# Moving matmul operands to 512-byte boundaries, joining a tile's scans, and spacing the convolution

## The chip, the cores and the metric

One core of a Trainium2 chip runs the whole program. The metric is the device time of one execution in microseconds, the median of three runs. Five engines work side by side: TensorE (PE; its weight loads are listed apart as PEld), VectorE (DVE), ScalarE (ACT), GpSimd (POOL) and SyncE (SP), which only issues DMAs here. A matmul has a stationary operand, which a weight load brings into the array, and a moving operand, which streams past it; both are read from SBUF. An address in SBUF is a byte offset inside each of the 128 partitions.

## The reference, cut to what matters

The layer is two SwiGLU feed-forward blocks around a mixer, on 256 tokens of 2048 channels, all in float32:

```python
x = x + 0.5 * swiglu(rms_norm(x, g1), w1, w3, w2)      # w1, w3: 2048x5632, w2: 5632x2048
h = rms_norm(x, gm);  p = h @ w_in                     # q|k, v, o, gates, u
qk = silu(causal_depthwise_conv(qk, conv_w, conv_b))   # 4 taps, 1024 channels
hm = mlstm_chunkwise(q, k, v, i, f);  hm = rms_norm(hm) * sigmoid(o)
bu = einsum('bsgh,gph->bsgp', u, b_bar)                # 64 groups of 16 channels, 64 states each
states = associative_scan(combine, (lam_bar, bu))      # s[t] = lam_bar * s[t-1] + bu[t]
y = gelu(real(einsum(states, c)) + d * u);  hs = y * sigmoid(y @ w_glu + b_glu)
x = x + concat(hm, hs) @ w_out
x = x + 0.5 * swiglu(rms_norm(x, g2), v1, v3, v2)
out = rms_norm(x, gf)
```

## The kernel before

Every large product is done in three matmuls on pairs of float32r numbers. A weight tile arrives as float32 in `wraw`; ACT rounds it to `whi` (line 154), DVE forms the rest `wlo = wraw - whi` (line 156), and activations are split the same way into `xh`/`xl`, `gh`/`gl`, `hmh`/`hml`, `yh`/`yl` and `hsh`/`hsl`. The product is then hi·hi + hi·lo + lo·hi.

The work is cut into weight steps. One step is 512 KB of weights (two blocks of 128 rows by 512 columns) and one call of `step_tok` or a quarter to an eighth of `gemm_ch`. In `step_tok` (line 174) the activation is stationary and the weight is moving: 12 matmuls of 512 columns. In `gemm_ch` (lines 224 to 226) the weight is stationary and the activation moves, 256 columns at a time: 24 matmuls. Three steps are prepared ahead (`AHEAD`), through four `wraw`, three `whi` and three `wlo` buffers.

The stages in order: feed-forward 1 (`w1`, `w3` from `xh`/`xl`, then `w2` from `gh`/`gl`, in two halves of 6 and 5 chunks), the mixer, feed-forward 2 in the same form. The last column block of the last `w2` is done by `tail`, with 256-column matmuls on lines 474 to 476. The mixer's products are, in order: `u` (two chunks, `gemm_ch`), `o` and the gates (three chunks of 344 columns), `q|k` (two chunks, `gemm_ch`), `v` (two chunks), the first half of `w_out` from `hmh`/`hml`, `w_glu` from `yh`/`yl` (`gemm_ch`), and the second half of `w_out` from `hsh`/`hsl`.

Beside the products of the mixer runs the S5 branch, in eight tiles of four scan rows. Each tile is six tasks: load (DMAs of its tables on SP's queue), drive (16 small matmuls, then four DVE products by the rotation table and two POOL sums), scan (line 860), unrotate (six POOL operations, lines 868 to 873), emit (matmuls and one DVE operation), act (ACT and DVE). The tasks wait in the list `self.bg`; after each weight step `tick` runs 0.62 of one on average (`S5_RATE`). The convolution and other short pieces are put in by `self.after(n, fn)`: `fn` is recorded after the n-th weight step from then. SP's order is the recorded one; the order on the other engines is made by a scheduler from the recorded program.

The tiles lie one after another in SBUF, in the order in which the pools are opened, so each tile's address follows from the sizes of those before it. As the two programs are built, the starts of TensorE's operands, modulo 512 bytes, are:

| operand | where it is used | before | changed |
|---|---|---|---|
| `xh`, `xl` | stationary in `w1`, `w3`, `o`, `v`; moving in `u`, `q\|k` | 256 | 0 |
| `whi`, `wlo` | moving in `step_tok` and `tail`, stationary in `gemm_ch` | 256 | 0 |
| `gh`, `gl` | stationary in `w2` and `tail` | 320 | 0 |
| `hsh`, `hsl` | stationary in the second half of `w_out` | 352 | 0 |
| `hmh`; `hml` | stationary in the first half of `w_out` | 32; 96 and 0 | 0 |
| `yh`, `yl` | moving in `w_glu` | 352 | 0 |

Within a tile the slices step by 512 or 1024 bytes in the stationary operand and by 1024 or 2048 in the moving one (1376 in the 344-column chunks, whose second block so starts at 96 before). `xh` and `whi` lie below byte 96,000 of a partition; all the other operands of the table lie above 114,000, before and after.

Of the kernel before, what the change touches and what calls it, by code (L numbers as in the profile page):

```python
# [8 lines left out]
F32 = mybir.dt.float32  # L9
# [28 lines left out]
AHEAD = 2  # L38
WARM = 7
# [20 lines left out]
class _Layer:  # L60
# [172 lines left out]
    def setup(self):  # L233
# [16 lines left out]
        vec0 = self.junkp.tile([KD, P], F32, name="vec0")  # L250
# [3 lines left out]
        idle = self.junkp.tile([P, NC], F32, name="junk")  # L254
# [8 lines left out]
        self.mhalf = c.tile([P, 8], F32, name="mhalf")  # L263
# [6 lines left out]
        vecs = self.junkp.tile([rows, P], F32, name="vecs")  # L270
# [500 lines left out]
    def mixer(self, chunk_done):  # L771
# [4 lines left out]
        with ExitStack() as ctx:  # L776
            mp = self.pool("mix", ctx=ctx)
# [7 lines left out]
            def make_rB():  # L785
                b = self.bank()
                for t in range(TT):
                    dg = tp2.tile([P, P], F32, name="dg")
                    V.tensor_scalar(dg, self.ident, rstd(t), None, op0=ALU.mult)
                    nc.tensor.matmul(b[:, t * P:(t + 1) * P], lhsT=self.ones, rhs=dg, start=True, stop=True)  # L790
# [5 lines left out]
            uT = [mp.tile([P, 4, 2, HC], F32, name=f"uT{i}", tag=f"uT{i}") for i in range(2)]  # L796
            u4 = [mp.tile([P, 8, HC], F32, name=f"u4{i}", tag=f"u4{i}") for i in range(2)]
# [14 lines left out]
            yT = mp.tile([P, NJ, S], F32, name="yT")  # L812
            yh = mp.tile([P, NJ, S], F32R, name="yh")
            yl = mp.tile([P, NJ, S], F32R, name="yl")
# [7 lines left out]
            def s5(j):  # L822
# [3 lines left out]
                def load():  # L826
# [9 lines left out]
                    Bt = [mp.tile([P, 4, HC], F32, name=f"B{i}") for i in range(2)]  # L836
                    env["t"] = rv, w1, w2, k0, At, Bt

                def drive():
                    rv, w1, w2, k0, At, Bt = env["t"]  # L840
# [15 lines left out]
                def scan():  # L856
                    rv, w1, w2, k0, At, Bt = env["t"]
                    for a in (0, 2):
                        for q in range(4):
                            V.tensor_tensor_scan(At[a + 1][:, q, :],  # L860
                                                 self.R[:, 4 * j + q:4 * j + q + 1].broadcast_to([P, HC]),
                                                 At[a][:, q, :], 0.0, op0=ALU.mult, op1=ALU.add)

                def unrotate():
                    rv, w1, w2, k0, At, Bt = env["t"]
                    cs, sn = rv[:, 0], rv[:, 1]
                    zr, zi = At[1], At[3]
# [7 lines left out]
                def emit():  # L875
                    rv, w1, w2, k0, At, Bt = env["t"]
# [51 lines left out]
            for i, part in enumerate(self.gates(mp, gt, Dm, em)):  # L928
# [24 lines left out]
            for hf in range(2):  # L953
                acc = self.pair()
                self.gemm_ch(acc, self.xs, win, KD, QK0 + hf * NC)
                qkp[hf] = mp.tile([P, 4, S + 3], F32, name=f"qkp{hf}", tag=f"qkp{hf}")
# [4 lines left out]
                for i in range(4):  # L961
                    self.after(1 + i, lambda hf=hf, i=i: conv(hf, i))
# [37 lines left out]
            def heads_T(c):  # L1000
                hmh[c] = mp.tile([P, 4, S], F32R, name=f"hmh{c}", tag=f"qkp{c}")
                hml[c] = mp.tile([P, 4, S], F32R, name=f"hml{c}", tag=f"vx{c}")
# [15 lines left out]
            for c in range(2):  # L1018
                v = mp.tile([P, TT, 2, DV + 1], F32, name=f"vx{c}", tag=f"vx{c}")
# [37 lines left out]
            hsh = [mp.tile([P, 4, S], F32R, name=f"hsh{i}", tag=f"uT{i}") for i in range(2)]  # L1057
            hsl = [mp.tile([P, 4, S], F32R, name=f"hsl{i}", tag=f"u4{i}") for i in range(2)]
# [26 lines left out]
    def gates(self, mp, gt, Dm, em):  # L1085
# [3 lines left out]
        rows = mp.tile([H, 4, S], F32, name="g_rows", tag="vx1")  # L1089
        more = mp.tile([H, 4, S], F32, name="g_more", tag="qkp1")  # L1090
        E = mp.tile([H, NCK, S], F32, name="g_E", tag="vx0")
# [130 lines left out]
```

## Time and profile before

| | |
|---|---|
| median of 3 runs | 1885.29 us (1884.81 to 1885.33) |
| the profiled execution | 1883.44 us, of which the profile's span is 1881.7 us |
| PE busy | 1840.2 us, 9221 matmuls |
| DVE busy | 1082.8 us, 1335 instructions |
| ACT, POOL busy | 811.5 us, 340.3 us |
| clock granted to TensorE | 0.995 of full speed on average |

A matmul's duration in the profile runs to the modelled end of its pipeline, so consecutive matmuls overlap and a busy PE may still be slower than it could be. What a matmul costs in a dense stretch is the time from its start to the next one's start; the timeline gives it.

### The profile page before, as it was taken

The page shows a single profiled execution, that of the slowest core. Times are in us where ns is not written, and L with a number is a line of the kernel's source. Part 1 is how long each engine was busy: PE and PEld are TensorE (multiplying, and loading weights), DVE is VectorE, ACT ScalarE, POOL GpSimd, SP SyncE. Part 2 cuts the span into 40 slices and gives each one's busy share as a digit, 9 for nine tenths or more (in the row PEclk, how much of TensorE's full clock was granted, in tenths as well). Part 3 has the DMA queues.
Part 4 walks back from the last instruction along what each step waited for, and adds up shares of the span by engine and source line. Part 5 has one row for each costly group of instructions (what it writes and reads, how often), then busy time and mean ns, then how long its engine had stood idle before and what let it go on. Part 6 is the DMA issues. An engine that isn't in the chain of part 4 may idle for free.

```text
span 1881.7 us, 24161 instructions
## 1 busy us (share of the span) xinstructions
PE 1840.2 (98%) x9221; PEld 1539.7 (82%) x9221; DVE 1082.8 (58%) x1335; ACT 811.5 (43%) x970; POOL 340.3 (18%) x523
## 2 busy tenths in 40 slices
PE   9999999999999999988889999999999999999998
PEld 7888888888888888987778888888888888888887
DVE  5547865555555455577888765445444444444454
ACT  6444443334444444434544455444443334444343
POOL 3000999700000000166323200000000000000011
PEclk9999999999999999999999999999999999999999
DMA  8666666666666555776766556666665566666554
GB/s 261 190 189 188 200 208 216 236 197 201 189 194 197 186 194 189 206 156 179 158 155 178 168 178 204 190 190 190 190 190 185 187 188 190 190 190 190 190 188 148
DMA packets 191252, 358.27 MB, mean 190 GB/s; under 512 B 12320, under 2 KB 29344, under 8 KB 191008
## 3 DMA queue, kind: packets, MB, share of 16 engines
q1 hardware_dynamic: 186992, 344.58, 62.2%
q0 software_dynamic: 4000, 11.10, 1.8%
q8 instruction: 72, 1.18, 0.3%
q10 hardware_dynamic: 144, 1.05, 0.1%
q14 instruction: 44, 0.36, 0.1%
HBM read 344.62 MB, written 11.01 MB: 189 GB/s over the span
## 4 chain that ended last, share of the span: by engine, by line
PE 48%; DVE 5%; issue 1%; DMA 1%; ACT 1%; POOL 0%; ACTq 0%; POOLq 0%; DVEq 0%
PE accb L174 42%; DVE wlo L156 2%; DVE A L860 1%; PE accb L226 1%; PE accb L224 1%; PE accb L225 1%; DMA wraw<-in_w_in_dram 1%; DVE qkc L942 1%; PE tpb L486 1%; PE accb L474 0%; PE accb L476 0%; PE accb L475 0%; DVE qkc L939 0%; ACT whi L154 0%; PE tpb L845 0%
## 5 line engine op out<-in xcount | busy, mean ns | idle before, releaser
L156 DVE TENSOR_TENSOR wlo<-wraw,whi 128x1024 fp32r<-128x1024 f32 (+1 forms) x630 | 788.6, 1254 | 736.6 <-ACT whi L154 736.0
L154 ACT CAST whi<-wraw 128x1024 fp32r<-128x1024 f32 (+1 forms) x630 | 655.0, 1041 | 950.9 <-PE accb L174 856.9
L174 PE MATMUL accb<-wlo,xh 128*128 128x512 f32 (+1 forms) x1568 | 606.2, 387 | 17.1 <-DVE wlo L156 17.1
L174 PE MATMUL accb<-whi,xh 128*128 128x512 f32 (+1 forms) x1568 | 609.7, 389 | 0.0
L174 PE MATMUL accb<-whi,xl 128*128 128x512 f32 (+1 forms) x1568 | 605.6, 387 | 0.0
L174 PEld LDWEIGHTS accb<-wlo,xh 128*128 128x128 f32 x1568 | 296.0, 189 | 76.4 <-DVE wlo L156 20.1
L174 PEld LDWEIGHTS accb<-whi,xl 128*128 128x128 f32 x1568 | 296.2, 189 | 57.9
L174 PEld LDWEIGHTS accb<-whi,xh 128*128 128x128 f32 x1568 | 295.9, 189 | 58.0 <-ACT whi L154 1.1
L174 PE MATMUL accb<-whi,gh 128*128 128x512 f32 x664 | 263.7, 397 | 0.0
L174 PE MATMUL accb<-whi,gl 128*128 128x512 f32 x664 | 262.4, 395 | 0.0
L174 PE MATMUL accb<-wlo,gh 128*128 128x512 f32 x664 | 262.3, 395 | 0.0
L174 PEld LDWEIGHTS accb<-whi,gl 128*128 128x128 f32 x664 | 124.7, 188 | 30.2
L174 PEld LDWEIGHTS accb<-whi,gh 128*128 128x128 f32 x664 | 124.7, 188 | 29.7
L174 PEld LDWEIGHTS accb<-wlo,gh 128*128 128x128 f32 x664 | 124.7, 188 | 29.6
L1186 POOL TENSOR_TENSOR x<-x,fn 128x512 f32<-128x512 f32 x6 | 8.9, 1500 | 699.6 <-ACT junk L317 699.6
L696 POOL TENSOR_TENSOR tr<-s5rot,sp 128x128 f32<-128x128 f32 (+6 forms) x112 | 62.1, 555 | 151.9 <-DVE sp L636 148.4
L226 PE MATMUL accb<-xh,wlo 128*128 128x256 f32 x256 | 73.6, 288 | 6.6 <-DVE wlo L156 6.6
L224 PE MATMUL accb<-xh,whi 128*128 128x256 f32 x256 | 73.9, 289 | 0.0
L225 PE MATMUL accb<-xl,whi 128*128 128x256 f32 x256 | 73.0, 285 | 0.0
L757 POOL DMA_DIRECT2D spillw<-s5w x16 | 8.6, 541 | 274.6 <-ACT s5w L728 259.7
L697 POOL TENSOR_TENSOR tr<-s5rot,sp 128x128 f32<-128x128 f32 (+6 forms) x112 | 57.8, 517 | 0.0
L226 PEld LDWEIGHTS accb<-xh,wlo 128*128 128x128 f32 x256 | 49.6, 194 | 7.6 <-DVE wlo L156 7.6
(312 smaller groups left out, 1416.3 us busy)
## 6 DMA issues: line engine op xcount, KB each, us to landing
wraw<-in_ffn_w_dram SPq DMA_DIRECT2D x528, 512.0 KB, 3.7
wraw<-in_w_in_dram SPq DMA_DIRECT2D x48, 512.0 KB, 5.3
wraw<-in_w_out_dram SPq DMA_DIRECT2D x32, 512.0 KB, 3.7
wraw<-in_w_in_dram SPq DMA_DIRECT2D x24, 344.0 KB, 5.6
spillrot<-s5rot POOLq DMA_DIRECT2D x8, 512.0 KB, 5.3
spillw<-s5w POOLq DMA_DIRECT2D x16, 256.0 KB, 4.2
s5rot<-spillrot SPq DMA_DIRECT2D x8, 512.0 KB, 7.8
wraw<-in_w_glu_dram SPq DMA_DIRECT2D x8, 512.0 KB, 3.9
```

Source lines behind the costliest of these rows:

```text
L154: nc.scalar.copy(hi, raw)
L156: nc.vector.tensor_sub(lo, raw, hi.bitcast(F32))
L174: nc.tensor.matmul(acc[t][:, :n], lhsT=x, rhs=wt, start=first and t not in seen, stop=last and t not in left)
L224: nc.tensor.matmul(o, lhsT=wh[:, kk, ns], rhs=xh, start=st, stop=False, **kw)
L225: nc.tensor.matmul(o, lhsT=wh[:, kk, ns], rhs=xl, start=False, stop=False, **kw)
L226: nc.tensor.matmul(o, lhsT=wl[:, kk, ns], rhs=xh, start=False, stop=sp, **kw)
L486: nc.tensor.transpose(b[:, o:o + P], s[t][:, kt * P:(kt + 1) * P], self.ident)
L696: G.tensor_tensor(tr[0][:, :, :k], rv[:, 0, :, 0:k], u0, op=ALU.mult)
L697: G.tensor_tensor(tr[1][:, :, :k], rv[:, 1, :, 0:k], u1, op=ALU.mult)
L860: V.tensor_tensor_scan(At[a + 1][:, q, :], self.R[:, 4 * j + q:4 * j + q + 1].broadcast_to([P, HC]), At[a][:, q, :], 0.0, op0=ALU.mult, op ...
L942: V.scalar_tensor_tensor(o, src[:, w:w + S], self.col("conv_w", w * 8 + j), o, op0=ALU.mult, op1=ALU.add)
L1186: nc.gpsimd.tensor_tensor(self.x[c][:, t, :], self.x[c][:, t, :], self.fn[:, c * NC:(c + 1) * NC], op=ALU.mult)
```

## The change

All operands of TensorE in the table above are moved to addresses that are whole multiples of 512. Small paddings (`mhalf`, `junk`) shift the early pools; two early vectors move from the junk pool into S5 buffers; in the mixer a pool `ma` for the operands is opened first, the tiles `qkp` and `vx`, whose buffers later hold `hmh` and `hml`, are padded to 1152 numbers, and the rest goes to `mp`. The S5 tile's scan becomes one instruction over its four rows, in place, with a tile `Rt` as the multiplier that ACT fills in the load task and whose first column in each row is zero, so that a row starts anew. Unrotate takes the two freed tiles as its scratch, and `B0`, `B1` go. The convolution's four tiles of a chunk are recorded after weight steps 1, 3, 5, 7 and not 1, 2, 3, 4.

```diff
+WIDE = 1152
...
-        vec0 = self.junkp.tile([KD, P], F32, name="vec0")
+        vec0 = self.s5p.tile([KD, P], F32, name="vec0", tag="s5k0")
...
-        idle = self.junkp.tile([P, NC], F32, name="junk")
+        idle = self.junkp.tile([P, NC + 112], F32, name="junk")[:, :NC]
...
-        self.mhalf = c.tile([P, 8], F32, name="mhalf")
+        self.mhalf = c.tile([P, 72], F32, name="mhalf")[:, :8]
...
+            ma = self.pool("mixa", ctx=ctx)
             mp = self.pool("mix", ctx=ctx)
...
-            uT = [mp.tile([P, 4, 2, HC], F32, name=f"uT{i}", tag=f"uT{i}") for i in range(2)]
+            uT = [ma.tile([P, 4, 2, HC], F32, name=f"uT{i}", tag=f"uT{i}") for i in range(2)]
...
+            Rt = [mp.tile([P, 4, HC], F32, name=f"Rt{i}") for i in range(2)]
+            for i in range(2):
+                G.memset(Rt[i][:, :, 0:1], 0.0)
...
-                    Bt = [mp.tile([P, 4, HC], F32, name=f"B{i}") for i in range(2)]
-                    env["t"] = rv, w1, w2, k0, At, Bt
+                    A.copy(Rt[j % 2][:, :, 1:],
+                           self.R[:, 4 * j:4 * j + 4].unsqueeze(2).broadcast_to([P, 4, HC - 1]))
+                    env["t"] = rv, w1, w2, k0, At
...
                     for a in (0, 2):
-                        for q in range(4):
-                            V.tensor_tensor_scan(At[a + 1][:, q, :],
-                                                 self.R[:, 4 * j + q:4 * j + q + 1].broadcast_to([P, HC]),
-                                                 At[a][:, q, :], 0.0, op0=ALU.mult, op1=ALU.add)
+                        x = At[a].rearrange("p q c -> p (q c)")
+                        V.tensor_tensor_scan(x, Rt[j % 2].rearrange("p q c -> p (q c)"), x, 0.0,
+                                             op0=ALU.mult, op1=ALU.add)
...
-                    zr, zi = At[1], At[3]
+                    zr, zi, Bt = At[0], At[2], (At[1], At[3])
...
-                qkp[hf] = mp.tile([P, 4, S + 3], F32, name=f"qkp{hf}", tag=f"qkp{hf}")
+                qkp[hf] = ma.tile([P, WIDE], F32, name=f"qkp{hf}", tag=f"qkp{hf}")[:, :4 * (S + 3)].rearrange("p (j s) -> p j s", j=4)
...
-                    self.after(1 + i, lambda hf=hf, i=i: conv(hf, i))
+                    self.after(1 + 2 * i, lambda hf=hf, i=i: conv(hf, i))
```

TensorE's order is that of before. On DVE the first place is the second chunk of `q|k`, where the convolution of the first chunk stands between the `wlo` steps; `qkc` is written by a convolution tile's four operations, and `yT` is S5's emit. Before:

```order
L156 TENSOR_TENSOR wlo_8061<-wraw_8057,whi_8059 128x1024
L939 TENSOR_SCALAR qkc_7626<-qkp0_7972,cols_130 128x256
L888 SCALAR_TENSOR_TENSOR yT_6406<-uT0_6402,cols_130,tpb_8092 128x256
L942 SCALAR_TENSOR_TENSOR qkc_7626<-qkp0_7972,cols_130,qkc_7626 128x256
L156 TENSOR_TENSOR wlo_8115<-wraw_8111,whi_8113 128x1024
L942 SCALAR_TENSOR_TENSOR qkc_7626<-qkp0_7972,cols_130,qkc_7626 128x256
L939 TENSOR_SCALAR qkc_7626<-qkp0_7972,cols_130 128x256
L942 SCALAR_TENSOR_TENSOR qkc_7626<-qkp0_7972,cols_130,qkc_7626 128x256 x2
L156 TENSOR_TENSOR wlo_8150<-wraw_8146,whi_8148 128x1024
```

The same place on DVE in the changed program:

```order
L157 TENSOR_TENSOR wlo_8082<-wraw_8078,whi_8080 128x1024
L945 TENSOR_SCALAR qkc_7605<-qkp0_7950,cols_130 128x256
L157 TENSOR_TENSOR wlo_8117<-wraw_8113,whi_8115 128x1024
L948 SCALAR_TENSOR_TENSOR qkc_7605<-qkp0_7950,cols_130,qkc_7605 128x256
L945 TENSOR_SCALAR qkc_7605<-qkp0_7950,cols_130 128x256
L948 SCALAR_TENSOR_TENSOR qkc_7605<-qkp0_7950,cols_130,qkc_7605 128x256 x3
L157 TENSOR_TENSOR wlo_8153<-wraw_8149,whi_8151 128x1024
```

Between the three `wlo` steps there stood two and four operations of the convolution, and now one and five; the next steps have four, none and two.

On ACT the second place is the end of the second `u` chunk: the casts of that chunk (128x1024) and of the first `o` chunk (128x688). Before:

```order
L340 ACTIVATE xh_6479<-tpb,cols 128x256 x4
L154 CAST whi<-wraw 128x1024 x11
L154 CAST whi<-wraw 128x688 x8
L892 ACT_TABLE_LOAD
L892 ACTIVATE yT<-yT 128x256
```

And in the changed program, where `Rt` is the scan's multiplier:

```order
L341 ACTIVATE xh_6486<-tpb,cols 128x256 x4
L155 CAST whi<-wraw 128x1024 x11
L842 COPY Rt_6416<-R 128x4x127
L155 CAST whi<-wraw 128x688 x7
L842 COPY Rt_6417<-R 128x4x127
L155 CAST whi<-wraw 128x688
L898 ACT_TABLE_LOAD
```

The third of the eight copies into `Rt` stands in front of the casts of the `o` chunk; it writes the buffer that the first tile's scan on DVE reads, and the casts behind it follow in order.

## Rows read from the trace of the kernel before

**Rows 1.** page: span, busy time, clock and GB/s by slices, chain by engine

```profile
span 1881.7 us, 24161 instructions
...
PEclk9999999999999999999999999999999999999999
...
GB/s 261 190 189 188 200 208 216 236 197 201 189 194 197 186 194 189 206 156 179 158 155 178 168 178 204 190 190 190 190 190 185 187 188 190 190 190 190 190 188 148
...
PE 48%; DVE 5%; issue 1%; DMA 1%; ACT 1%; POOL 0%; ACTq 0%; POOLq 0%; DVEq 0%
```

**Rows 2.** groups by shape on PE: line, operands, count; busy us, mean ns; idle

```profile
L174 PE MATMUL accb<-whi,xh 128*128 128x512 f32 x1472 | 577.4, 393 | 0.0
...
L174 PE MATMUL accb<-whi,gh 128*128 128x512 f32 x664 | 263.7, 397 | 0.0
...
L174 PE MATMUL accb<-whi,hsh 128*128 128x512 f32 x64 | 25.6, 400 | 0.0
...
L474 PE MATMUL accb<-whi,gh 128*128 128x256 f32 x48 | 13.3, 276 | 0.0
...
L474 PE MATMUL accb<-xh,gh 128*128 128x256 f32 x32 | 8.8, 276 | 0.0
```

**Rows 3.** timeline of PE (start, us, engine, line), feed-forward 2, w1 and w3

```profile
1169.79 0.39 PE L174 MATMUL accb<-whi,xl 128*128 128x512 f32 x1
...
1171.15 0.39 PE L174 MATMUL accb<-whi,xl 128*128 128x512 f32 x1
```

**Rows 4.** timeline of PE, feed-forward 2, w2

```profile
1499.72 0.40 PE L174 MATMUL accb<-whi,gh 128*128 128x512 f32 x1
...
1501.12 0.40 PE L174 MATMUL accb<-whi,gh 128*128 128x512 f32 x1
```

**Rows 5.** timeline of PE, tail

```profile
1859.81 0.28 PE L475 MATMUL accb<-wlo,gh 128*128 128x256 f32 x1
...
1860.49 0.28 PE L475 MATMUL accb<-xl,gh 128*128 128x256 f32 x1
```

**Rows 6.** timeline of PE, u chunk (gemm_ch)

```profile
774.81 0.28 PE L225 MATMUL accb<-xl,whi 128*128 128x256 f32 x1
...
775.53 0.28 PE L225 MATMUL accb<-xl,whi 128*128 128x256 f32 x1
```

**Rows 7.** timeline of PE after its longest wait in the v chunk

```profile
975.12 0.63 PE L174 MATMUL accb<-whi,xl 128*128 128x512 f32 x1
...
976.82 0.63 PE L174 MATMUL accb<-whi,xh 128*128 128x512 f32 x1
```

**Rows 8.** windows: stretch, us, PE busy (count), granted clock, DMA share, GB/s

```profile
974.50:977.00 2.50, 2.48 (x6) 0.50 0.42 66
```

**Rows 9.** waits of PE in 785 to 985 us: total us, times, longest

```profile
PE accb L174 <- DVE wlo L156: 16.3, 9, 5.1
PE accb L226 <- DVE wlo L156: 6.6, 5, 2.9
```

**Rows 10.** windows: stretch, us, busy of PE, PEld, DVE, ACT, POOL, clock

```profile
920.00:980.00 60.00, 48.32 (x328) 41.93 (x328) 54.41 (x82) 27.89 (x35) 24.65 (x18) 0.94 0.53 137
```

**Rows 11.** groups by shape on DVE, 760 to 1110 us

```profile
L860 DVE TENSOR_TENSOR_SCAN A<-R,A 128x128 f32<-128x128 f32 x64 | 36.7, 636 | 2.6 <-POOL A L853 2.6
...
L1115 DVE TENSOR_TENSOR_SCAN g_rows<-g_more,g_rows 4x256 f32<-4x256 f32 x1 | 0.7, 678 | 0.0
```

**Rows 12.** timeline of POOL: end of the first unrotate

```profile
815.13 1.79 POOL L873 TENSOR_TENSOR S<-B,B 128x512 f32<-128x512 f32 x1
```

**Rows 13.** timeline of DVE: first scans, and the second drive

```profile
802.97 4.79 DVE L860 TENSOR_TENSOR_SCAN A<-R,A 128x128 f32<-128x128 f32 x8
...
818.36 0.68 DVE L849 TENSOR_TENSOR A<-tpb,s5rot 128x512 f32<-128x512 f32 x1
```

**Rows 14.** groups by shape on ACT: a copy of 128x512

```profile
L724 ACT COPY s5w<-tpb 128x512 f32<-128x512 f32 x8 | 4.6, 579 | 0.0
```

**Rows 15.** timeline of ACT: first cast of the o chunk

```profile
805.23 0.77 ACT L154 CAST whi<-wraw 128x688 fp32r<-128x688 f32 x1 [1.83 <-PE accb L225]
```

More of the change, by code (lines that the diff above doesn't have):

```diff
@@ L269, in setup @@
         rows = 16 + 16 + 32 + 8 * 4
-        vecs = self.junkp.tile([rows, P], F32, name="vecs")
+        vecs = self.s5p.tile([rows, P], F32, name="vecs", tag="s5k0")
         r = 0
@@ L793, in mixer @@
             self.after(7, make_rB)
-            uT = [mp.tile([P, 4, 2, HC], F32, name=f"uT{i}", tag=f"uT{i}") for i in range(2)]
-            u4 = [mp.tile([P, 8, HC], F32, name=f"u4{i}", tag=f"u4{i}") for i in range(2)]
+            uT = [ma.tile([P, 4, 2, HC], F32, name=f"uT{i}", tag=f"uT{i}") for i in range(2)]
+            u4 = [ma.tile([P, 8, HC], F32, name=f"u4{i}", tag=f"u4{i}") for i in range(2)]
             def evac_u(hf, acc):
@@ L927, in mixer @@
             em = mp.tile([P, TT, H], F32, name="em")
-            for i, part in enumerate(self.gates(mp, gt, Dm, em)):
+            for i, part in enumerate(self.gates(ma, mp, gt, Dm, em)):
                 self.after(1 + 4 * i, part)
@@ L1000, in heads_T @@
             def heads_T(c):
-                hmh[c] = mp.tile([P, 4, S], F32R, name=f"hmh{c}", tag=f"qkp{c}")
-                hml[c] = mp.tile([P, 4, S], F32R, name=f"hml{c}", tag=f"vx{c}")
+                hmh[c] = ma.tile([P, 4, S], F32R, name=f"hmh{c}", tag=f"qkp{c}")
+                hml[c] = ma.tile([P, 4, S], F32R, name=f"hml{c}", tag=f"vx{c}")
                 for half in range(2):
@@ L1054, in mixer @@
             self.drain_bg()
-            hsh = [mp.tile([P, 4, S], F32R, name=f"hsh{i}", tag=f"uT{i}") for i in range(2)]
-            hsl = [mp.tile([P, 4, S], F32R, name=f"hsl{i}", tag=f"u4{i}") for i in range(2)]
+            hsh = [ma.tile([P, 4, S], F32R, name=f"hsh{i}", tag=f"uT{i}") for i in range(2)]
+            hsl = [ma.tile([P, 4, S], F32R, name=f"hsl{i}", tag=f"u4{i}") for i in range(2)]
             def evac_glu(hf, acc):
@@ L1083, in mixer, with gates @@
                 chunk_done(c)
-    def gates(self, mp, gt, Dm, em):
+    def gates(self, ma, mp, gt, Dm, em):
         nc = self.nc
         V, G, A = nc.vector, nc.gpsimd, nc.scalar
-        rows = mp.tile([H, 4, S], F32, name="g_rows", tag="vx1")
-        more = mp.tile([H, 4, S], F32, name="g_more", tag="qkp1")
-        E = mp.tile([H, NCK, S], F32, name="g_E", tag="vx0")
+        rows = ma.tile([H, 4, S], F32, name="g_rows", tag="vx1")
+        more = ma.tile([H, 4, S], F32, name="g_more", tag="qkp1")
+        E = ma.tile([H, NCK, S], F32, name="g_E", tag="vx0")
         li, f, bc, M = (rows[:, i, :] for i in range(4))
```

18 lines of the change are left out of this document (9 added, 9 removed).

## The prediction

> **What bounds the kernel now.** I read the page first: the chain of waits gives PE 48% of its own and hardly anything to the others, and TensorE's clock is granted in full in all forty slices [rows 1]. So outside the mixer only two things can shorten the program, fewer matmuls or matmuls that follow each other sooner; PE's order and its number of matmuls stay. Then I took the groups of PE by shape, for the counts [rows 2], and the timeline of PE in dense stretches, for the time from one matmul's start to the next one's, which is what a matmul costs there.
>
> At the full clock of 2.4 GHz, 512 columns at one column a cycle would take 213.3 ns and 256 columns 106.7 ns. The timeline shows more, and not the same everywhere. Stationary `xh`/`xl` with moving weights: six matmuls in 1171.15 - 1169.79 = 1.36 us, 226.7 ns each [rows 3]. Stationary `gh`/`gl`: six in 1.40 us, 233.3 ns [rows 4]. The tail, 256 columns on `gh`: six in 0.68 us, 113.3 ns [rows 5]. `gemm_ch`, 256 columns: six in 0.72 us, 120 ns [rows 6]. At the half clock there is no excess: four matmuls in 1.70 us are 425 ns, against 512/1.2 = 426.7 ns [rows 7, 8]. So at the full clock something costs 13.3 or 20 ns a matmul, and it differs with the operands. That is what this change can act on.
>
> Last I read the waits of PE in the mixer: between 785 and 985 us it waits 16.3 + 6.6 us for `wlo` of DVE [rows 9], DVE being busy 54.4 of the 60 us from 920 on while the granted clock falls to 0.94 [rows 10]. There, and only there, what DVE does counts.
>
> **The change part by part.** The sum is made against the profiled 1883.44 us; the median is 1885.29, so 1.85 are added at the end.
>
> *Operands that are in step already.* In `w1`, `w3` and `v` both operands start at 256 modulo 512, in `gemm_ch` of `u` and `q|k` too; afterwards both start at 0. Two readings of the rows are possible. By the first, the excess depends on how the stationary start stands to the moving start: 256 against 256 costs 13.3 ns, `gh` at 320 against weights at 256 costs 20. Then 0 against 0 is 256 against 256, and the 4416 matmuls (3 x 1472 [rows 2]) stay at 226.7. By the second, the excess is paid for operands that do not start on a line of 512, and it goes. Ends: 0 and -13.3 x 4416 = -58.9 us; for `gemm_ch`, 768 matmuls (4 chunks x 8 steps x 24), 0 and -10.2. I take 0 for both. The reason is the tail beside `gemm_ch`: the tail's stationary start, 320, is out of step with the moving 256 and it has the shorter distance, 113.3 against 120, while with 512 columns out of step is the longer. Being off the line is common to all four rows, so it cannot make the difference between them; the pairing can.
>
> *Operands that come into step.* `gh`/`gl`, 3 x 664 = 1992 matmuls of 512 columns [rows 2], go from 320 against 256 to 0 against 0, so by the first reading from 233.3 to 226.7: -6.7 x 1992 = -13.3 us. Ends: 0 (the difference comes from where in SBUF `gh` lies, above byte 114,000, which it keeps) and -20 x 1992 = -39.8 (the second reading). `hsh`/`hsl`, 3 x 64 = 192, and `hmh`/`hml`, also 192 and partly on the line already, have no dense rows of their own; out of step like `gh`, I give them its price, and half of it for `hm`, where one tile starts at 0: -1.3 and -0.6; ends 0 and -20 x 384 = -7.7. The tail, 3 x (48 + 32) = 240 matmuls of 256 columns [rows 2], goes the other way by this reading, from 113.3 to the 120 of the pairs in step: +1.6; other end -1.6. `yh` in `w_glu` (192) and the three chunks of 344 columns, whose second block started at 96, I leave at 0; other end about -7 ns x 192 and, at 13.3 ns, 288 matmuls of the latter: -5.2 together.
>
> *Scans.* Now eight scans a tile, 64 in all with a mean of 636 ns; the first eight stand in one row of 4.79 us [rows 11, 13]. Afterwards two of 512 elements. The only longer scan, 256 elements, took 678 ns [rows 11]; twice that for 512 is 1.36, so two take 2.7 us if nothing else holds them. But a scan of 128 elements should take less than the 256-element one by far more than 636 against 678 shows: part of the mean is waiting inside the instruction, which I expect to remain. Ends per tile: 0 and 4.79 - 2.7 = -2.1 us of DVE, over eight tiles -16.6 of DVE's time. Of that only what lies ahead of a late `wlo` reaches PE, at most the 22.9 us of waits [rows 9] together with the next part. I take 0.
>
> *Copies into `Rt`.* Eight on ACT, each near the 128x512 copy of 579 ns [rows 14]: 4.6 us of an engine that is busy 27.9 of 60 us [rows 10]. But the third stands in front of the casts of the `o` chunk and must wait until the first tile's scans have read the buffer; they ended at 802.97 + 4.79 = 807.76, and the first of these casts started at 805.23 [rows 13, 15]. It would be late by 2.5 us, plus the copy. Queued behind it are `whi`, then `wlo`, then PE, with three steps prepared ahead, each of 12 matmuls of 344 columns here. I take 0 for all; the price without this cover is a rival below. Unrotate's scratch is now `At[1]` and `At[3]`, so the next drive waits for POOL's last read of them: before, POOL ended at 815.13 + 1.79 = 816.92 and the drive's first product started at 818.36 [rows 12, 13], 1.4 us to spare. Cost 0; if the cover goes, what POOL is late by, at most a microsecond or two a tile.
>
> *Convolution.* Four tiles of four operations go to every second step. In the second `q|k` chunk DVE has one, five, four, none and two of them between `wlo` steps where it had two, four, four, one and one: nearly the same clumps. The fourth tile goes where steps are empty, and in the `v` chunk, which holds the longest wait [rows 9], tasks of S5 stand beside it. Ends: +3 (the longer clump) and half of the 22.9 us of waits, -11.5. I take -4, a third of the better end, since one tile in four changes its place by much.
>
> Sum: -13.3 - 1.3 - 0.6 + 1.6 - 4 = -17.6; 1883.4 - 17.6 = 1865.8, and with 1.85 as a median 1867.7. Forecast: 1868 us.
>
> The supply of weights does not stop this: a step of 512 KB in 12 x 213.3 ns = 2.56 us wants 205 GB/s, and the first slice moved 261 [rows 1].
>
> **A rule of the Trainium skill.** The page "TensorE: Matmul & The Clock Gate", section "Back-to-back issue gap", gives N/2.4 + 2.5 ns for a matmul alone at the full clock: 215.8 ns for 512 columns and 109.2 for 256. The trace disagrees, with 226.7 and 233.3, 120 and 113.3 [rows 3 to 6]; if the excess over that rule is what alignment costs, rival A would end near 1785 instead of the time worked out for it below. The page "SBUF — State Buffer", section "Specifications (TRN2)", gives lines of 16 bytes and a penalty for each crossing. All the starts of before are multiples of 16, so by it moving them is worth nothing, which is rival C; the difference of 226.7 and 233.3 between two multiples of 16 speaks against it.
>
> **The rivals.**
> A: the line decides, and on it the whole excess goes. FFN with `xh`, 4224 x 13.3 = 56.3 (4416 less the 192 of `v`); `gh` 39.8; `hs` 3.8; tail 1.6; in the mixer, where PE waits for DVE in part, I count about 8 of the 17 to 20 that the ends above allow; with the convolution 113.5. 1883.4 - 113.5 + 1.85 = 1772. For it: no excess at the half clock, so reading cannot keep up, as it would with split lines. Against it: 256 columns out of step are quicker than in step.
> B: half of the excess goes, one operand's share: (109.5)/2 + 4 = 59, so 1826.
> C: what differs is the place in SBUF, or nothing in the starts; then only the convolution acts: 1885.3 - 4 = 1881, and 1885 if that does nothing either. For it: `xh` lies low and `gh` high.
> S, slower: the copies into `Rt` hold the casts. The third to eighth each wait for the scan of two tiles before, up to 2.5 us, and all take ACT's time: 6 x 2.5 + 8 x 0.58 = 19.6 us. If half of it reaches PE and the starts give nothing, 1885.3 + 9.8 = 1895. It decides as soon as a copy is later than the three prepared steps last, 12 matmuls of 344 columns each; PE's waits for `wlo` show that this lead is often used up already [rows 9].
>
> **How the numbers follow.** Forecast 0.45, A 0.22, B 0.10, C 0.12, S 0.11. The measurement can tell about 0.2% from no change, 3.8 us. Faster: forecast, A, B and a quarter of C, 0.80; same: most of C, 0.09; slower: S, 0.11. The range goes from A's 1772 to C's 1884; left out are S and the far side of A. The forecast's own range is 1860 to 1876, from the ends of the convolution and of `hs`, `hm` and the tail.
>
> **What will show it.** In the timeline of PE: `gh` at 226.7 ns and `xh` still at 226.7 is the forecast; both at about 213 is A, both near 220 B, 233 and 227 C. The tail at 120 or 113 tells whether pairing or being out of step matters at 256 columns. In the mixer: the waits for `wlo` between 785 and 985 us below 20 us, the scan's mean by shape near 2.3 us if the waiting inside it remains and 1.4 if not, and the cast after the third copy no later than before. The forecast is wrong if `xh` changes its distance, and wrong in the other way if `whi` waits for `Rt`.

## The result and the profile after

The changed kernel took 1860.21 us, the median of 4 runs (1858.73 to 1863.14), against 1885.31 for the kernel before on the same chip (4 runs, 1884.81 to 1887.8). The ratio is 0.9868, with a 95% interval of 0.9856 to 0.9880: 1.3% faster, 25.1 us where 17.3 were forecast. The execution that was profiled took 1863.14 us, 20.3 less than that of before.

From the page of the changed kernel, each engine's busy time in us, its share of the span and its instructions:

```profile
PE 1828.1 (98%) x9221; PEld 1540.8 (83%) x9221; DVE 1077.2 (58%) x1287; ACT 814.8 (44%) x977; POOL 347.6 (19%) x525
```

PE has the same 9221 matmuls. Where the time went is read by stages. This table is worked out from the starts in both traces: from a stage's first matmul to the first of the next, in us.

| stage | before | after | difference |
|---|---|---|---|
| feed-forward 1 and 2, `w1`/`w3` (four stretches) | 272.12, 224.79, 266.53, 221.23 | 272.79, 224.77, 266.48, 221.17 | +0.5 |
| `w2` without the tail (four stretches) | 137.52, 117.77, 135.28, 84.88 | 133.85, 114.77, 131.45, 82.49 | -12.9 |
| tail | 27.10 | 28.67 | +1.6 |
| `u` | 51.52 | 50.34 | -1.2 |
| `o` and gates, 344 columns | 68.92 | 69.64 | +0.7 |
| `q\|k` | 67.71 | 61.71 | -6.0 |
| `v` | 65.14 | 63.76 | -1.4 |
| first half of `w_out`; `w_glu`; second half | 54.47; 23.03; 47.58 | 53.56; 23.03; 46.23 | -0.9; 0; -1.4 |

The timeline of PE in the dense stretches of the changed kernel (start and duration in us), in the order `u`, `w1`/`w3`, `w2`, tail:

```profile
774.76 0.28 PE L226 MATMUL accb<-xl,whi 128*128 128x256 f32 x1
...
775.48 0.28 PE L226 MATMUL accb<-xl,whi 128*128 128x256 f32 x1
...
1169.88 0.39 PE L175 MATMUL accb<-whi,xl 128*128 128x512 f32 x1
...
1171.24 0.39 PE L175 MATMUL accb<-whi,xl 128*128 128x512 f32 x1
...
1479.88 0.39 PE L175 MATMUL accb<-whi,gl 128*128 128x512 f32 x1
...
1481.24 0.39 PE L175 MATMUL accb<-whi,gl 128*128 128x512 f32 x1
...
1840.04 0.28 PE L475 MATMUL accb<-xh,gh 128*128 128x256 f32 x1
...
1840.76 0.28 PE L475 MATMUL accb<-xh,gh 128*128 128x256 f32 x1
```

Each pair spans six matmuls. `xh` takes 1.36 us, 226.7 ns each, as before [rows 3]. `gh` takes 1.36 where it took 1.40 [rows 4], so 226.7 and not 233.3. The tail takes 0.72 where it took 0.68 [rows 5], 120 and not 113.3 ns, and `gemm_ch` 0.72 as before [rows 6]. This holds for whole stages and not only for the pairs shown. Worked out from all starts in both traces, without the distances that hold a wait, the means are: `w2` 233.3 before and 226.8 after, `w1`, `w3` and the other products of `xh` 226.9 in both, the tail 113.4 and 120.0.

In the mixer, the waits of PE in 785 to 985 us (us in all, times, the longest):

```profile
PE accb L175 <- DVE wlo L157: 14.6, 12, 3.4
...
PE accb L175 <- ACT whi L155: 1.5, 3, 0.8
PE accb L227 <- DVE wlo L157: 1.4, 4, 0.8
```

Against [rows 9] the waits for `wlo` fell from 22.9 to 16.0 us, 5.2 of it in `gemm_ch` (6.6 to 1.4), and a small wait for `whi` is new. The groups of DVE in 760 to 1110 us hold the scans:

```profile
L867 DVE TENSOR_TENSOR_SCAN A<-Rt,A 128x512 f32<-128x512 f32 x16 | 28.7, 1820 | 2.6 <-POOL A L860 2.6
```

They keep DVE busy for 28.7 us and not 36.7 [rows 11]. The means hide two kinds of scan. The shortest, median and longest in ns, before and after:

```profile
L860 DVE TENSOR_TENSOR_SCAN A<-R,A x64: 391/394/1518, 803.0 to 1039.8; 128x128 f32<-128x128 f32 x64
L867 DVE TENSOR_TENSOR_SCAN A<-Rt,A x16: 1192/2282/2317, 796.6 to 1024.1; 128x512 f32<-128x512 f32 x16
```

Of the 64 scans before, 14 took 1.44 to 1.52 us and nearly all others 0.39 to 0.42. Of the 16 joined ones, 9 took 2.27 to 2.32 and the others 1.19 to 1.22. In both traces every long one overlaps a `tensor_tensor` of POOL (lines 854 and 868 before, 861 and 874 after) by 1.16 us or more, and none of the short ones by more than 1.04. So a long scan holds a wait of about 1.1 us: there were 14 such waits and there are 9. A scan without one also costs less when joined, 1.19 us where four took 4 x 0.39 = 1.57.

On ACT, the copies into `Rt` wait for scans as the order suggested; first the waits of ACT in 740 to 1000 us, then its timeline at the third copy:

```profile
ACT Rt L842 <- DVE A L867: 20.8, 5, 6.0
```

```profile
800.10 0.61 ACT L842 COPY Rt<-R 128x508 f32<-128x508 f32 x1 [3.03 <-DVE A L867]
800.62 0.76 ACT L155 CAST whi<-wraw 128x688 fp32r<-128x688 f32 x1
```

ACT stood still for 20.8 us behind five copies, 3.0 of it before the cast at 800.62. PE waits for `whi` for only 1.5 us, and in starts_alone (below), which has no copies, it waits for 1.2 us. A `wlo` that is late because its `whi` was late would stand under `wlo`; the waits don't part the two. POOL's last read of the unrotate scratch, and DVE's next drive:

```profile
808.50 1.79 POOL L879 TENSOR_TENSOR S<-A,A 128x512 f32<-128x512 f32 x1
```

```profile
811.73 0.68 DVE L856 TENSOR_TENSOR A<-tpb,s5rot 128x512 f32<-128x512 f32 x1
```

The read ends at 810.29, 1.4 us ahead of the drive, the same slack as before [rows 12, 13].

### The profile page after: what moved, and what is told of

Read it like the earlier page. It is cut to its first block, busy times and chain, and to the rows that moved or that the text cites. A ratio compares the mean times of both kernels' runs of the same rounds, so it can differ in the third digit from the quotient of the medians.

```text
span 1861.4 us, 24119 instructions
## 1 busy us (share of the span) xinstructions
PE 1828.1 (98%) x9221; PEld 1540.8 (83%) x9221; DVE 1077.2 (58%) x1287; ACT 814.8 (44%) x977; POOL 347.6 (19%) x525
## 4 chain that ended last, share of the span: by engine, by line
PE 89%; DVE 5%; DMA 2%; issue 2%; POOL 1%; ACT 1%; SPq 0%; ACTq 0%; POOLq 0%; DVEq 0%
PE accb L175 81%; DVE wlo L157 2%; DMA wraw<-in_w_in_dram 1%; PE tpb L487 1%; PE accb L225 1%; PE accb L227 1%; PE accb L226 1%; DVE A L867 1%; PE tpb L336 1%; DMA s5rot<-spillrot 0%; POOL u L811 0%; DVE qkc L948 0%; PE accb L477 0%; PE accb L476 0%; PE accb L475 0%
## 5 line engine op out<-in xcount | busy, mean ns | idle before, releaser
L175 PE MATMUL accb<-whi,gh 128*128 128x512 f32 x664 | 259.7, 391 | 0.0
L175 PE MATMUL accb<-whi,gl 128*128 128x512 f32 x664 | 258.4, 389 | 0.0
L175 PE MATMUL accb<-wlo,gh 128*128 128x512 f32 x664 | 258.4, 389 | 0.0
L697 POOL TENSOR_TENSOR tr<-s5rot,sp 128x128 f32<-128x128 f32 (+6 forms) x112 | 65.6, 587 | 151.9 <-DVE sp L637 148.4
L699 POOL TENSOR_TENSOR s5rot<-tr,tr 128x128 f32<-128x128 f32 (+6 forms) x112 | 60.2, 549 | 3.3
```

The source lines that it names most:

```text
L175: nc.tensor.matmul(acc[t][:, :n], lhsT=x, rhs=wt, start=first and t not in seen, stop=last and t not in left)
L697: G.tensor_tensor(tr[0][:, :, :k], rv[:, 0, :, 0:k], u0, op=ALU.mult)
L699: G.tensor_tensor(rv[:, a, :, k:2 * k], tr[0][:, :, :k], tr[1][:, :, :k], op=op)
```

## The experiments

Below, the difference of two operands means the stationary start less the moving start.

**phase_grid.** Only the matmuls, with the starts set one by one:

```diff
+        for i in range(16):
+            for j in range(16):
+                section(mov[i], sta[j], 512, 4)
```

> The distance of matmuls by itself: none of the layer is computed. Constants in SBUF, no DMA and no other engine beside TensorE, twelve matmuls of one shape in a row per section, in the pattern of the kernel's (stationary 0 with moving 0, stationary 0 with moving 1, stationary 1 with moving 0), for 16 starts of the moving and 16 of the stationary operand, 32 bytes apart modulo 512, with 512, 256 and 344 columns; stationary tiles below byte 96,000 and a second set above 114,000. Theory 1 (the distance follows the difference of the two starts, modulo 512): with 512 columns 226.7 ns for every pair with equal starts, at 0 and off the line alike, 233.3 where the stationary start is 64 bytes on; with 256 columns 120 for equal starts and 113.3 at 64 on; the low and the high set the same. Other differences were not seen and may give other values, down to 213.3 and 106.7. Rival (the line): at 0 and 0 the least, and any pair off the line 13 to 20 ns more. Rival (place in SBUF): 226.7 for the low set and 233.3 for the high one whatever the starts.

The timeline of PE shows a section of twelve matmuls in one row; the letter is the start in units of 32 bytes (`ma` is 0 and `mc` 64; `sc` is 64, `sd` 96, `sk` 320; `hi` is 256 in the set above byte 114,000):

```profile
120.11 2.89 PE L56 MATMUL accb<-mc,sc 128*128 128x512 f32 x12
122.84 2.95 PE L56 MATMUL accb<-mc,sd 128*128 128x512 f32 x12
125.63 2.96 PE L56 MATMUL accb<-mc,se 128*128 128x512 f32 x12
...
142.37 2.89 PE L56 MATMUL accb<-mc,sk 128*128 128x512 f32 x12
145.10 2.95 PE L56 MATMUL accb<-mc,sl 128*128 128x512 f32 x12
...
760.20 2.89 PE L56 MATMUL accb<-ma,hi 128*128 128x512 f32 x12
762.92 1.32 PE L56 MATMUL accb<-ma,hj 128*128 128x512 f32 x5
```

Equal starts: (122.84 - 120.11)/12 = 227.5 ns; 32 bytes on: 2.79/12 = 232.5. And 256 bytes on, `sk`, it is 2.73/12 = 227.5 again: the pattern repeats after 256 bytes, not 512. The high set is as fast: (762.92 - 760.20)/12 = 226.7. Worked out from the eleven distances inside each section of twelve, as the median over the sections of the low set (all but the first, in which matmuls still followed each other at 427 ns):

| difference modulo 256 | 0 | 32 | 64 | 96 | 128 | 160 | 192 | 224 |
|---|---|---|---|---|---|---|---|---|
| ns, 512 columns | 226.6 | 232.9 | 233.5 | 233.5 | 231.7 | 233.5 | 229.8 | 233.4 |

Every row of the grid shows these values, shifted, within 3 ns. Line and place both fall: 0 against 0 is not better than 64 against 64. Twelve matmuls are few, though: at 128 the longer sections of phase_fine (below) gave 233.5 and not 231.7, and with 256 columns the grid gave 117 to 120 ns for all differences, which is not what longer sections give.

**gh_at_64.** One part undone: the difference of `gh` that before had.

```diff
-        idle = self.junkp.tile([P, NC + 112], F32, name="junk")[:, :NC]
+        idle = self.junkp.tile([P, NC + 128], F32, name="junk")[:, :NC]
```

> The changed kernel with 64 bytes more of padding ahead of the pools that hold gh and the mixer's operands, so that gh, gl, hm, hs, yh and yl start at 64 modulo 512 while xh and whi stay at 0: the difference that gh had before. Theory 1 (difference of the starts): gh and hs at 233.3 ns again, the tail at 113.3, so +13.3 + 1.3 + 1.3 - 1.6 = +14.3 us, 1874 to 1875 us. Rival (the gain of w2 is the place in SBUF or less traffic beside it): gh stays at 226.7, 1860 us.

1875.02 us (0.9947 of before, 0.9932 to 0.9961), 14.8 us above the changed kernel. Its timeline of PE, `w2` and tail:

```profile
1479.65 0.39 PE L175 MATMUL accb<-whi,gl 128*128 128x512 f32 x1
...
1481.05 0.39 PE L175 MATMUL accb<-whi,gl 128*128 128x512 f32 x1
...
1854.80 0.28 PE L475 MATMUL accb<-xh,gh 128*128 128x256 f32 x1
...
1855.48 0.28 PE L475 MATMUL accb<-xh,gh 128*128 128x256 f32 x1
```

Both old distances are back, 233.3 and 113.3 ns, from 64 bytes of padding alone.

**all_at_128.** No operand on a line of 512, the differences as in the changed kernel:

```diff
-        self.mhalf = c.tile([P, 72], F32, name="mhalf")[:, :8]
+        self.mhalf = c.tile([P, 104], F32, name="mhalf")[:, :8]
```

> The changed kernel with 128 bytes more of padding in the first pool: every operand of TensorE starts at 128 modulo 512, none on a whole line, and the differences stay 0. Theory 1 (the difference decides): every distance as in the changed kernel, 1860 us. Rival (whole 512-byte lines): each stationary slice now lies on two lines, w2 at 233 ns, so 1874 us or more.

1862.05 us (0.9876, 0.9860 to 0.9893), beside 1860.81 for **changed_again** in the same job, whose interval (0.9852 to 0.9882) overlaps. `w2` on PE:

```profile
1479.93 0.39 PE L175 MATMUL accb<-whi,gl 128*128 128x512 f32 x1
...
1481.29 0.39 PE L175 MATMUL accb<-whi,gl 128*128 128x512 f32 x1
```

226.7 ns. Whole lines are not what `w2` gained from.

**changed_again.** The changed kernel, unedited.

> The changed kernel itself, beside the others on the same chip: 1860 us by every theory, so that the single reversals can be set against it.

It repeated. In its trace the `o` chunks took 67.42 us where the first trace has 69.64, with the same code: a difference of 2 us in the `o` chunks means nothing by itself. (Most of it is the clock, granted at 0.98 of full speed there in the first trace and at 1.00 in this one.) `q|k` is steadier: 61.71 in the first trace, 61.69 here, 61.68 in all_at_128 and 61.79 in gh_at_64.

**conv_1234, scans_apart, starts_alone.** The other two parts, undone singly and together. The first two edits, of which the third is the sum:

```diff
-                    self.after(1 + 2 * i, lambda hf=hf, i=i: conv(hf, i))
+                    self.after(1 + i, lambda hf=hf, i=i: conv(hf, i))
```

```diff
-                    A.copy(Rt[j % 2][:, :, 1:],
-                           self.R[:, 4 * j:4 * j + 4].unsqueeze(2).broadcast_to([P, 4, HC - 1]))
...
-                        x = At[a].rearrange("p q c -> p (q c)")
-                        V.tensor_tensor_scan(x, Rt[j % 2].rearrange("p q c -> p (q c)"), x, 0.0,
-                                             op0=ALU.mult, op1=ALU.add)
+                        for q in range(4):
+                            V.tensor_tensor_scan(At[a][:, q, :],
+                                                 self.R[:, 4 * j + q:4 * j + q + 1].broadcast_to([P, HC]),
+                                                 At[a][:, q, :], 0.0, op0=ALU.mult, op1=ALU.add)
```

> The changed kernel with the convolution's tiles at weight steps 1, 2, 3, 4 again, all else as changed. Theory 1: the 7.4 us that the q|k and v chunks gained come from the spacing, so this takes 1860 + 7 = 1867 us, and the wait for wlo in the second q|k chunk is back at 5 to 6 us. Rival: they come from the scans in one instruction (fewer DVE instructions beside the same chunks); then 1860 to 1862.

> The changed kernel with each tile's scans as eight instructions of one row again, in place, without the copies of the multiplier on ScalarE. Theory 1: the scans in one instruction were worth about nothing (forecast 0), 1859 to 1862 us. Rival (the gain of q|k and v comes from them): 1865 to 1867 us.

> The changed kernel with both other parts undone, the convolution at steps 1, 2, 3, 4 and eight scans a tile without the copies into Rt: only the starts are moved. Theory 1 (the starts are worth what the forecast's terms say, 13.6 us, and the mixer gains the rest by DVE's relief, the two reliefs sharing the same waits): 1870 us, less than the sum of the two single reversals would give (1860.2 + 6.6 + 6.1 = 1873). Rival (the two are independent): 1873. Rival (the starts help the mixer too): 1866.

| | median, us | ratio to before | `q\|k` in its trace, us | of it PE idle, us | granted clock in it |
|---|---|---|---|---|---|
| starts_alone | 1870.49 | 0.9921 (0.9906 to 0.9936) | 68.81 | 8.9 | 0.93 |
| conv_1234 (starts, scans) | 1866.78 | 0.9903 (0.9888 to 0.9918) | 65.72 | 5.9 | 0.92 |
| scans_apart (starts, spacing) | 1866.35 | 0.9909 (0.9893 to 0.9926) | 65.24 | 6.7 | 0.95 |
| changed_again (all) | 1860.81 | 0.9867 (0.9852 to 0.9882) | 61.69 | 4.1 | 0.97 |

PE's idle time is the stage less PE's busy time, here for starts_alone and changed_again (stretch; its length and PE's busy time in us; granted clock, DMA share, GB/s):

```profile
874.34:943.15 68.81, 59.94 (x491) 0.93 0.70 163
872.20:933.89 61.69, 57.64 (x490) 0.97 0.75 170
```

The waits of PE for `wlo` in 785 to 985 us, in the order starts_alone, conv_1234, scans_apart:

```profile
PE accb L175 <- DVE wlo L157: 16.7, 9, 5.1
PE accb L227 <- DVE wlo L157: 6.3, 4, 2.9
```

```profile
PE accb L175 <- DVE wlo L157: 15.0, 9, 4.0
PE accb L227 <- DVE wlo L157: 3.3, 3, 2.9
```

```profile
PE accb L175 <- DVE wlo L157: 14.3, 9, 5.1
PE accb L227 <- DVE wlo L157: 4.1, 3, 2.2
```

The starts alone take away none of the mixer's waiting (23.0 us for `wlo`, against 22.9 before). Spacing and joined scans each take 3 to 4 us off `q|k`, and together 7.1 us there (68.81 to 61.69) and 9.7 in the medians. So both theories of one cause alone fall: each of the two is about half of it. The wait for `wlo` in `gemm_ch` that conv_1234 was to bring back to 5 to 6 us came back to 3.3.

My reason for part of the 1870 of starts_alone, that the reliefs share the same waits, is not borne out either; the time came out at 1870.49 because the starts are worth what their terms say. The reliefs add up, in `q|k` (3.1 + 3.6 = 6.7 against 7.1) and over the four stages from `u` to `v`: 253.99 us in starts_alone, 249.68 in conv_1234, 249.56 in scans_apart, and with both 243.62 in changed_again and 245.45 in the first trace (4.3 + 4.4 = 8.7 against 10.4 and 8.5). The medians are too coarse for a sum. They have 3.7 + 4.1 = 7.8 against 9.7, but the kernel before took 1883.68 us beside conv_1234 and scans_apart and 1885.20 beside the other two. By the ratios it is 3.4 + 2.3 against 10.2, and each ratio is known only to 0.15%, 2.8 us, so whether there is more than the sum is open.

Not all of the gain in `q|k` is waiting. PE's idle time falls there by 3.0 us with the joined scans alone, by 2.2 with the spacing alone and by 4.8 with both. The other 2.3 of the 7.1 us are busy time that goes with the granted clock: 59.94 us at 0.93 and 57.64 at 0.97 are nearly the same work, 55.7 and 55.9 us at full speed. Before, `q|k` had 9.9 us of idle time at a clock of 0.97, so against that kernel the gain of 6.0 is nearly all idle time. Whether the lower clocks belong to their kernels or to the one execution that was traced is not shown.

**phase_fine.** Steps of 4 bytes, fewer stationary and fewer moving columns:

```diff
+        for d in range(64):
+            section(d, 512, 8)
...
+        for d in (0, 16):
+            for cols in (96, 64, 32):
+                section(d, 512, 8, cols)
```

> Matmuls by themselves again, none of the layer computed, one moving tile at 0 modulo 512 and the stationary operand 0 to 252 bytes on in steps of 4 bytes, sections of 24 matmuls with 512 columns and 48 with 256; then with 96, 64 and 32 stationary columns, and with 448 to 128 moving columns, at 0 and at 64 bytes. Theory 1 (the reading of the stationary operand for the next matmul takes turns from the moving one's, and their difference decides how many): fewer stationary columns shorten the 226.7 ns towards 213.3, with 64 columns to about 220; with fewer moving columns the excess of 13.3 stays. At differences that are no multiple of 32 bytes the distance lies between 226.7 and 236, and none is below 226.7. Rival (a fixed cost of each matmul): 226.7 whatever the stationary columns. Rival (there is a better start than an equal one): some step of 4 bytes gives 220 or less.

A section is 24 matmuls; less the last one's 0.39 us, 23 distances stand in its row. The rows are 204 bytes on, and 64 and 32 stationary columns at equal starts:

```profile
305.69 5.61 PE L42 MATMUL accb<-m,s 128*128 128x512 f32 x24
...
749.11 5.68 PE L42 MATMUL accb<-m,s 128*64 128x512 f32 x24
754.63 5.72 PE L42 MATMUL accb<-m,s 128*32 128x512 f32 x24
```

The theory's explanation fell: with 64 and 32 stationary columns the distance is 230 and 232 ns, not shorter but longer than 226.6. (At 64 bytes on, 96 columns gave 229 where 128 gave 233: there fewer columns were a little quicker.) No step of 4 bytes went below 226.6 with 512 columns (the range is 226.6 to 237.7, where the theory had at most 236), so no start that was tried is better than an equal one; some odd ones, 204 among them, are as good. With 448, 384 and 320 columns the excess over one column a cycle was 16, 13 and 13 ns; with 192 and 128 columns the distance was 112 ns for both, so there the pair of weight load and matmul has a floor. With 256 columns, in sections of 48, 64 bytes on is 113.3 and equal is 120.0, as in the tail before and after. But 28, 32 and 36 bytes on took 133.3 throughout; the section at 32:

```profile
424.09 6.57 PE L42 MATMUL accb<-m,s 128*128 128x256 f32 x48
```

In phase_pairs (below) the same difference of 32, with the moving start at 224, took 118.3.

**weights_at_52.** An attempt to have both: by the sections, 204 bytes on is 226.6 with 512 columns, and its reverse, 52, is 113.3 with 256. `wlo` is shifted in the same way, and paddings put the activations on multiples of 256.

```diff
+LAG = 13
...
-        hi = self.whi.tile([P, KK * NC], F32R, name="whi")[:, :kk * n]
+        hi = self.whi.tile([P, KK * NC + 64], F32R, name="whi")[:, LAG:LAG + kk * n]
```

> The changed kernel with whi and wlo 52 bytes past a multiple of 256 and every activation on a multiple of 256 (a start 204 bytes on from the weights when stationary; 52 the other way round in gemm_ch). By the sections with matmuls alone 512 columns at 204 take 226.6 ns, as at 0, and 256 columns at 52 take 113.3 and not 120. Theory 1 (the difference decides, in the whole kernel as by itself): step_tok stays at 226.7, gemm_ch goes to 113.3: u 384 x 6.7 = 2.6 us, w_glu 192 x 6.7 = 1.3, of the 2.6 of q|k at most that much since PE waits for DVE there: 1860.8 - 4 to 6.5 = 1854 to 1857 us. Rival (what matmuls do alone at such a start doesn't hold beside DMA and the other engines, or odd starts of wlo slow DVE): no gain, 1861 or more.

1903.51 us, slower than before (1.0106, 1.0091 to 1.0122). Its timeline of PE in `w_glu` and in `w1`/`w3`:

```profile
1084.82 0.28 PE L226 MATMUL accb<-yh,whi 128*128 128x256 f32 x1
...
1085.50 0.28 PE L226 MATMUL accb<-yh,whi 128*128 128x256 f32 x1
...
1190.00 0.39 PE L176 MATMUL accb<-whi,xh 128*128 128x512 f32 x1
...
1191.40 0.40 PE L176 MATMUL accb<-whi,xh 128*128 128x512 f32 x1
```

`gemm_ch` did go to 113.3 ns here, but `step_tok` to 233. The sections had 204 with the moving start at 0, the kernel has it with the moving start at 52: so the difference alone does not decide. Of the quicker `gemm_ch`, 1.2 us reached a stage, in `w_glu` (21.82 us for 23.03). `u` and `q|k` took 50.28 and 61.34, hardly less than in the changed kernel (50.34 and 61.71), though half of their distances were 114 ns or less.

**phase_pairs.** The same with the moving start varied too:

```diff
+        for m in range(64):
+            section(m, m, 512, 8)
+        for m in range(64):
+            section(m, (m + 51) % 64, 512, 8)
```

> Matmuls by themselves, none of the layer computed: starts in steps of 4 bytes again, now also of the moving operand. First the moving start 0 to 252 with the stationary one at 0, 512 columns; then both starts equal; then the stationary start 204 bytes on from the moving one, modulo 256; then the first again with 256 columns. What weights_at_52 left open: 204 on was 226.6 ns with the moving start at 0, and 233.6 in the whole kernel with the moving start at 52. Theory 1a (the difference decides only between starts on multiples of 32 bytes; on finer steps the starts themselves count): 52 against 0 takes 233 to 234 here too, and equal starts off a multiple of 32 are no longer all 226.7. Rival 1b (the difference decides everywhere, and the whole kernel changes it by its other traffic): 204 on is 226.6 for every moving start, equal starts are always 226.7.

The rows: moving and stationary at 32 and 32, 52 and 52; then 32 and 236, 52 and 0 (204 on in both):

```profile
424.83 5.62 PE L43 MATMUL accb<-m,s 128*128 128x512 f32 x24
452.66 5.80 PE L43 MATMUL accb<-m,s 128*128 128x512 f32 x24
781.46 5.61 PE L43 MATMUL accb<-m,s 128*128 128x512 f32 x24
809.17 5.82 PE L43 MATMUL accb<-m,s 128*128 128x512 f32 x24
```

Worked out from the starts: 226.6 and 235.1 with equal starts, 226.6 and 235.8 with 204 on. With equal starts the distance over the moving start is 226.6, 237.8, 232.3, 229.0, 233.4, 235.0, 233.4, 228.9 for 0, 4, ... 28 bytes and repeats from 32 on. At 204 on the values repeat after 32 in the same way, save at the moving start 0:

```profile
736.80 5.79 PE L43 MATMUL accb<-m,s 128*128 128x512 f32 x24
```

That is 234.4 ns, from the same starts modulo 512 that gave 226.6 in phase_fine, each over a whole section. So rival 1b falls, and theory 1a holds in that starts off a multiple of 32 count by themselves: the distance goes with the moving start modulo 32 and with the difference modulo 256. But these two don't decide wholly, as this pair and the 133.3 against 118.3 above show. What else does, other bits of the addresses or the section that ran before, no run parts. (My 233 to 234 for 52 against 0 was low: 235.8 here, 233.7 in the kernel.)

**s5_rate_by_time, conv_2468.** Two tries at what is left in the mixer.

```diff
-            self.rate = S5_RATE
+            self.rate = 0.9
             u_chunk(1)
+            self.rate = 0.42
...
+            self.rate = 0.68
             for hf in range(2):
                 acc = self.pair()
                 self.gemm_ch(acc, self.xs, win, KD, QK0 + hf * NC)
```

```diff
-                    self.after(1 + 2 * i, lambda hf=hf, i=i: conv(hf, i))
+                    self.after(2 + 2 * i, lambda hf=hf, i=i: conv(hf, i))
```

> The changed kernel with the rate of the S5 tasks set by how long a weight step is on TensorE: 0.9 a step in the second u chunk, 0.42 in the o chunks of 344 columns, 0.68 from q|k on, and not 0.62 throughout. Theory 1 (18 us of PE's standing still in the o chunks come from too many tasks on DVE per us of PE): the o chunks lose 6 us or more of it, u and q|k gain back 2 to 3: 1856 to 1858 us. Rival (the o chunks wait for the gates' and o's own work on DVE, or the tasks are only pushed on into q|k, where PE waits then): 1860 or more.

> The changed kernel with the convolution's tiles after weight steps 2, 4, 6, 8 of the next chunk, and not 1, 3, 5, 7. Theory 1 (it is the spacing by two that relieves DVE between the wlo steps): 1859 to 1862 us, q|k as in the changed kernel. Rival (it is the early first step that matters, since work piles up at the chunk's end): 1864 to 1867.

The waits of PE in s5_rate_by_time, 740 to 985 us:

```profile
PE accb L175 <- DVE wlo L157: 11.9, 10, 3.6
PE accb L227 <- DVE wlo L157: 6.4, 4, 3.7
PE tpb L852 <- DMA u<-uT: 3.8, 2, 1.9
```

1870.29 us (0.9931, 0.9918 to 0.9943): the `o` chunks took 63.63 us, 6.0 less than in the first trace (3.8 less than in changed_again), but `u` took 57.95 (50.34) and `q|k` 69.82 (61.71), and the four stages from `u` to `v` 252.75 (245.45). The waits for `wlo` in `gemm_ch` are back at 6.4 us, and waits of 3.8 us for a DMA of S5's are added (0.2 in the changed kernel). The tasks were only pushed to where PE waited for them again: the rival. conv_2468 took 1860.01 us (0.9871, 0.9854 to 0.9889), as the changed kernel, with `q|k` at 60.20. Its waits, 755 to 1010 us:

```profile
PE accb L175 <- DVE wlo L157: 13.4, 11, 3.4
...
PE accb L227 <- DVE wlo L157: 0.2, 1, 0.2
```

As far as these two places show, it is the spacing by two that counts, not which of the steps. No version beat the changed kernel.

## Why the prediction was right, and where it was off

- *Operands already in step, 0 us.* Right: 226.7 before and after, and 768 `gemm_ch` matmuls at 120. The reading by pairs was the right one of the two; the grid shows it for all starts on multiples of 32, and the other reading has all_at_128 against it. `yh` and the 344-column chunks, left at 0, gave nothing either: `w_glu` took 23.03 us before and after, and the chunks' second block, at 96 before, is at 352 now, which leaves its difference at 160 modulo 256.
- *`gh`, -13.3; `hs`, -1.3; `hm`, -0.6; tail, +1.6.* The stages gave -12.9, -1.4, -0.9 and +1.6, and gh_at_64 gave them back (+14.8 for a stated +14.3). starts_alone, 14.7 below before, is these terms by themselves (-13.6).
- *Scans, 0.* This is the first term that was mis-sized. I took part of the mean of 636 ns as waiting that would stay. DVE's busy time fell by 8.0 us, half of the end of 16.6, and the joined scans have a mean of 1.82 us, between the 1.4 and 2.3 that the prediction named. The wait of 1.1 us in a scan beside POOL did stay, but it comes once an instruction, so there are 9 of them and not 14; and the scans without one got shorter too. Undoing the joining cost 5.5 us; alone beside the starts it brought 3.7, and 4.3 in the traces' stages from `u` to `v`.
- *Convolution, -4.* 4.1 us beside the starts alone (4.4 in the stages), 6.0 when undone in the changed kernel. That it came so near is in part luck, since the term was set at a third of an end. Spacing and scans together were worth 9.7 us where the sum had 4 for both; that is why the time came out at 1860.2, at the low edge of the forecast's own 1860 to 1876. In the profiled pair the four stages from `u` to `v` gained 7.8 us, which is how a forecast of 17.6 for the profile became 20.3. The other 5 us between 20.3 and the 25.1 of the medians are the two profiled executions: that of before was 1.9 under its median, that of after 2.9 over.
- *Copies into `Rt`, 0.* The wait that rival S spoke of is there, 20.8 us on ACT, but PE's wait for `whi` is 1.5 us with the copies and 1.2 without them; no loss of S's kind is seen. *`Bt` reuse, 0*: the slack of 1.4 us stayed.
- *Rivals.* A and B: no distance moved by their terms. C: only in so far as the 512-byte line is indeed nothing; the starts do matter. One row was read too far: a 9 in the page's clock row means nine tenths or more, so the clock was not granted in full in all forty slices ([rows 8] has 0.50). No term of the sum rests on it. The Trainium skill's "TensorE: Matmul & The Clock Gate", section "Back-to-back issue gap", gives N/2.4 + 2.5 ns for a matmul alone, 215.8 ns for 512 columns; in the streams here no pair of starts that was tried reached it: 226.6 was the least. (The estimate by this rule for rival A, with 10.9 and 17.5 ns a matmul in place of 13.3 and 20, comes to about 1789 us and not to the prediction's 1785.) The 16-byte lines of the Trainium skill's "SBUF — State Buffer", section "Specifications (TRN2)", don't explain the distances either: equal starts at 16 took 233.4 ns and at 32 226.6.

Open is what makes the 13 ns that every pair keeps, and by what mechanism the starts act; fewer stationary columns did not shorten it at equal starts, which speaks against the simplest form of "the weight load takes so many turns".

## What to carry to other kernels

Before moving operands to round addresses, read the start-to-start distances by pair of operands and set them beside the difference of the two starts: here equal starts (modulo 256, on multiples of 32) were as good as aligned ones, and 64 bytes of padding moved 14.8 us either way. The best difference depends on the number of columns, so check the short products too, and vary both starts before trusting a value from one of them. Test the pair in the whole kernel as well: by sections alone, weights_at_52 was to gain 4 to 6.5 us, and it lost 43. Where PE waited for one engine's late product here, two small reliefs on that engine added up, but moving its work to another stage only moved the wait. Read the granted clock of a stage beside its waits before putting its whole gain down to either.

## What the hardware showed that was not expected

- The distance of 512-column float32r matmuls, each with its own weight load, lay between 226.6 and 240.1 ns once a section had settled at the full clock. It went with the moving start modulo 32 and the difference of the starts modulo 256, though not with these alone (226.6 and 234.4 from the same starts in two programs). A stationary operand above byte 114,000 did as well as one below 96,000.
- With 256 columns, 64 bytes on is the quicker (113.3) and equal the slower (120); with 512 columns it is the other way round (233.3 and 226.7). The slowest seen with 256 columns was 133.3, at 28, 32 and 36 bytes on.
- Fewer stationary columns (96, 64, 32) made a matmul of 512 moving columns 3 to 5 ns slower at equal starts, not quicker.
- 192 and 128 moving columns both take 112 ns from start to start.
- A scan of 512 elements takes 1.19 us and four of 128 take 1.57; beside a `tensor_tensor` of POOL that overlaps it by over 1.1 us, a scan of either length takes 1.1 us more.
